# Seven block products for eight in the up projection of a decoder trunk

## The chip, the cores and the metric

The kernel runs on one core of a Trainium2 chip. The metric is the device time of one execution in microseconds; lower is better. TensorE multiplies, VectorE (DVE) and ScalarE (ACT) do the elementwise work, GpSimd (POOL) and SyncE (SP) here mostly issue DMAs.

## What is computed

One decoder layer on 512 tokens of 2048 features. The change is in its last sub-layer, a gated MLP with a short causal convolution, and in what hands over to it; the attention, the gated delta rule and the cross-attention before it keep their code.

```python
def conv_ffn(h, w_up, conv_w, conv_b, w_down):          # h (1, 512, 2048), w_up (2048, 11264)
    u = causal_dwconv(h @ w_up, conv_w) + conv_b         # 3 taps along the tokens
    gate, up = jnp.split(u, 2, axis=-1)                  # 5632 features each
    return (jax.nn.silu(gate) * up) @ w_down             # w_down (5632, 2048)
...
x = x + memory_cross_attention(rmsnorm(x, xattn_norm), mem_n, w_xq, w_xkv, w_xo)
x = x + conv_ffn(rmsnorm(x, ffn_norm), w_up, ffn_conv, ffn_conv_bias, w_down)
return rmsnorm(x, final_norm)
```

## The kernel before

Features lie on the 128 partitions, tokens along the free dimension, so that a tile is 128 features x 512 tokens. float32 accuracy is had by splitting each operand into a high part (rounded to float32r, a ScalarE copy) and a low part (the rest, a VectorE subtraction): `split` for activations, `load_w` for weights. `mm3` then makes a product of three matmuls, high x high, high x low, low x high, with the weights as the stationary operand. `load_w` loads a unit of weights (128 x 8 blocks x 128, 512 KB) into a `raw` tile (four buffers) through the SP queue and splits it into a `wh` tile (three buffers). A dense product of one feature tile over 2048 features (`dense`) is two units, 16 blocks, 48 matmuls of 512 columns.

The matmuls stand in program order (`pinned` chains them). On the other engines and on the DMA queues a scheduler sets the order when the program is built. Each engine, and each queue, works in that order: an instruction that waits holds up all behind it.

The cross-attention's output projection (`xo_part`, `xo_out`) makes 16 tiles: sum with the residual in `x4`, split of `x4 * g_ffn` into `x3hl`, and the sum of squares for the norm, whose factor `rs` is applied to the results of the up projection. The residual tiles `x4` (8 tiles of two) stay in the pool `hlB`, `x3hl` (16 tiles) in `hlA`.

The MLP then runs in six groups of gate features, 8, 8, 8, 8, 8 and 4 tiles of the 44. For each tile `ffn_mm` multiplies gate and up, `ffn_act` applies the norm and the convolution, and silu(gate) * up is split into `ghl`, in SBUF. After each group `down` adds its part of the down projection to all 16 tiles of `x4`: for each tile one unit of weights, 24 matmuls. The last group works in two halves of the tokens (`h0`, `h1`, 256 columns), with the first three blocks of some tiles ahead of the last gate, and ends in the final norm and the stores.

Of the kernel before, what the change touches and what calls it, by code (L numbers as in the profile page):

```python
# [34 lines left out]
def trunk(ctx, tc, xT, memT, w_in, w_first, w_ba, w_out, w_xq, w_xkv, w_xo, w_up, w_down,  # L35
# [868 lines left out]
    def ffn_act(f, ps, tag):
        y = fp.tile([P, S + 2], F32, tag="y", name="y", bufs=2)
# [1 line left out]
        dve.tensor_tensor(y[:, 2:], ps, rs, ALU.mult)
# [1 line left out]
        c = fp.tile([P, S], F32, tag=tag, name="c", bufs=2)
# [39 lines left out]
    groups = [(0, 8), (8, 16), (16, 24), (24, 32), (32, 40), (40, 44)]
    gate_next = None  # L950
    for gi, (f0, f1) in enumerate(groups):
        last = gi == len(groups) - 1
        for f in range(f0, f1):
            pg_ = ffn_mm(f) if gate_next is None else gate_next
            gate_next = None
            if f == 0:
                pu_ = ffn_mm(FT + f)
                drain()
                pb.close()
                fp = open_pool(ctx, "fp")  # L960
                ssq = fp.tile([P, S], F32, name="ssq4")
            g = ffn_act(f, pg_, "gate")
            act.activation(g, g, AF.Silu)
            if f:
                pu_ = ffn_mm(FT + f)
            u = ffn_act(FT + f, pu_, "up")
            dve.tensor_tensor(g, g, u, ALU.mult)
            if f % 10 < 8:
                t = hlB.tile([P, 2, S], F32R, tag="hl", name="ghl")
            else:  # L970
                t = fp.tile([P, 2, S], F32R, tag="ghl", name="ghl", bufs=2)
            split(t[:, 0], t[:, 1], g)
            ghl[f] = hl(t)
# [116 lines left out]
```

## Time and profile before

| | |
|---|---|
| median of 3 runs | 2573.16 us (2572.33 to 2577.62) |
| the profiled execution: its own time, its span | 2573.16 us, 2571.3 us |
| granted TensorE clock, mean | 0.997 |
| TensorE busy | 2541.5 us, 99% |
| VectorE, ScalarE, GpSimd busy | 54%, 38%, 6% |
| DMA | 293.05 MB, mean 114 GB/s |

Busy shares are of the span, which is the stretch from the first to the last instruction. Matmuls overlap in a pipeline, so the duration of one (some 0.39 us) is longer than the distance between two; the distance is read from the chain of work that ended last. In the rows PE is TensorE, L90 is the line of all dense matmuls, L141 and L143 split weights, L128, L129, L131 and L132 split activations, L910 and L912 are the convolution.

### The profile page before, as it was taken

The page shows a single profiled execution, that of the slowest core. Times are in us where ns is not written, and L with a number is a line of the kernel's source. Part 1 is how long each engine was busy: PE and PEld are TensorE (multiplying, and loading weights), DVE is VectorE, ACT ScalarE, POOL GpSimd, SP SyncE. Part 2 cuts the span into 40 slices and gives each one's busy share as a digit, 9 for nine tenths or more (in the row PEclk, how much of TensorE's full clock was granted, in tenths as well). Part 3 has the DMA queues.
Part 4 walks back from the last instruction along what each step waited for, and adds up shares of the span by engine and source line. Part 5 has one row for each costly group of instructions (what it writes and reads, how often), then busy time and mean ns, then how long its engine had stood idle before and what let it go on. Part 6 is the DMA issues. An engine that isn't in the chain of part 4 may idle for free.

```text
span 2571.3 us, 31857 instructions
## 1 busy us (share of the span) xinstructions
PE 2541.5 (99%) x12108; PEld 2109.7 (82%) x12108; DVE 1380.4 (54%) x2529; ACT 968.4 (38%) x1637; POOL 158.3 (6%) x426
## 2 busy tenths in 40 slices
PE   9999999999999999999999999999999999999997
PEld 7888877888887888888888888888888888888887
DVE  6766566666665446764444544444435543444356
ACT  5645434545554335543322332233223321332135
POOL 1111022212201000000000000000000000000000
PEclk9999999999999999999999999999999999999999
DMA  5444443333335445332232223222222222222332
GB/s 204 131 140 130 135 143 106 117 108 111 108 111 193 147 151 189 105 109 99 99 98 95 94 99 99 94 95 98 99 96 94 98 99 96 94 98 99 97 102 81
DMA packets 93243, 293.05 MB, mean 114 GB/s; under 512 B 12209, under 2 KB 17649, under 8 KB 93089
## 3 DMA queue, kind: packets, MB, share of 16 engines
q1 hardware_dynamic: 68960, 238.06, 28.2%
q0 software_dynamic: 12544, 33.00, 4.4%
q10 hardware_dynamic: 11584, 19.96, 2.1%
q8 instruction: 95, 1.56, 0.2%
q14 instruction: 60, 0.48, 0.1%
HBM read 266.29 MB, written 24.67 MB: 113 GB/s over the span
## 4 chain that ended last, share of the span: by engine, by line
PE 68%; DVE 1%; DMA 0%; ACT 0%; issue 0%; DVEq 0%; POOLq 0%; SPq 0%; ACTq 0%
PE psg L90 28%; PE psd L90 23%; PE pss L90 17%; DMA raw<-in_w_down 0%; DVE x L926 0%; PE pss L93 0%; DMA m<-mixed 0%; DVE wl L143 0%; DVE c L912 0%; DVE mhl L129 0%; ACT wl L141 0%; ACT e L813 0%; DMA xo<-in_xT 0%; DVE ghl L129 0%; ACT mhl L128 0%
## 5 line engine op out<-in xcount | busy, mean ns | idle before, releaser
L141 ACT ACTIVATE wh<-raw 128x1024 fp32r<-128x1024 f32 x424 | 449.7, 1061 | 1039.0 <-PE psg L90 362.8
L143 DVE TENSOR_TENSOR wh<-raw,wh 128x512 fp32r<-128x512 f32 x848 | 552.1, 688 | 337.7 <-ACT wh L141 337.2
L90 PE MATMUL psd<-xhl,wh 128*128 128x512 f32 x1824 | 470.0, 402 | 0.0
L90 PE MATMUL psg<-x3hl,wh 128*128 128x512 f32 x1824 | 416.5, 389 | 0.0
L90 PEld LDWEIGHTS psg<-x3hl,wh 128*128 128x128 f32 x1824 | 342.5, 188 | 71.4 <-issue 0.5
L90 PEld LDWEIGHTS psd<-xhl,wh 128*128 128x128 f32 x1824 | 331.0, 189 | 62.3 <-issue 0.5
L90 PE MATMUL psd<-x3hl,wh 128*128 128x512 f32 x1200 | 274.1, 389 | 0.0
L90 PE MATMUL pss<-x3hl,wh 128*128 128x512 f32 x1200 | 274.1, 389 | 0.0
L90 PEld LDWEIGHTS psd<-x3hl,wh 128*128 128x128 f32 x1200 | 225.3, 188 | 46.7
L90 PEld LDWEIGHTS pss<-x3hl,wh 128*128 128x128 f32 x1200 | 225.3, 188 | 46.7
L90 PE MATMUL pss<-xhl,wh 128*128 128x512 f32 x864 | 204.5, 392 | 0.0
L90 PE MATMUL psg<-ghl,wh 128*128 128x512 f32 x816 | 189.3, 392 | 0.0
L90 PEld LDWEIGHTS pss<-xhl,wh 128*128 128x128 f32 x864 | 160.7, 188 | 33.7
L90 PEld LDWEIGHTS psg<-ghl,wh 128*128 128x128 f32 x816 | 153.2, 188 | 34.0
L912 DVE SCALAR_TENSOR_TENSOR c<-y,fcv,c 128x512 f32<-128x512 f32 x176 | 131.8, 749 | 4.0 <-ACT c L910 1.0
L90 PE MATMUL pss<-ghl,wh 128*128 128x512 f32 x552 | 128.6, 392 | 0.0
L90 PE MATMUL psd<-ghl,wh 128*128 128x512 f32 x552 | 128.4, 391 | 0.0
L90 PE MATMUL psd<-mhl,wh 128*128 128x512 f32 x528 | 121.8, 390 | 1.6 <-DVE mhl L129 1.1
L90 PEld LDWEIGHTS pss<-ghl,wh 128*128 128x128 f32 x552 | 103.6, 188 | 23.0
L90 PEld LDWEIGHTS psd<-ghl,wh 128*128 128x128 f32 x552 | 103.6, 188 | 22.9
L90 PEld LDWEIGHTS psd<-mhl,wh 128*128 128x128 f32 x528 | 98.9, 188 | 23.4 <-DVE mhl L129 1.8
L906 POOL MEMSET y<- 128x2 f32 x88 | 8.7, 99 | 1484.5 <-DVE c L912 1358.0
(297 smaller groups left out, 2362.1 us busy)
## 6 DMA issues: line engine op xcount, KB each, us to landing
raw<-in_w_up SPq DMA_DIRECT2D x176, 512.0 KB, 3.3
raw<-in_w_in SPq DMA_DIRECT2D x104, 512.0 KB, 3.5
raw<-in_w_down SPq DMA_DIRECT2D x88, 512.0 KB, 3.3
raw<-in_w_out SPq DMA_DIRECT2D x32, 512.0 KB, 3.3
raw<-in_w_xkv SPq DMA_DIRECT2D x16, 512.0 KB, 3.9
kqv<-c ACTq DMA_DIRECT2D x24, 256.0 KB, 3.6
kqv_t<-kqv POOLq DMA_DIRECT2D x16, 256.0 KB, 3.1
xo<-in_xT POOLq DMA_DIRECT2D x16, 256.0 KB, 3.6
```

Of the source, the lines that this page charges most:

```text
L90: pinned(nc.tensor.matmul(out, a, b, start=start, stop=stop), c)
L141: act.activation(parts[0], raw, AF.Copy)
L143: dve.tensor_tensor(parts[1][:, c], raw[:, c], parts[0][:, c].bitcast(F32), ALU.subtract)
L906: pool.memset(y[:, 0:2], 0.0)
L912: dve.scalar_tensor_tensor(c, y[:, j:j + S], w[:, j:j + 1], c, ALU.mult, ALU.add)
```

## The change

Take the matrix product of a gate tile and an up tile with x as one of 2 x 2 blocks: rows of the result are gate and up, the inner dimension is cut into its first and second 1024 features, the tokens into their first and second 256. A11, A12 are the two units of the gate's weights, A21, A22 those of the up tile's. Strassen's scheme in Winograd's form needs seven block products (p1 to p7) where the plain product has eight, and 15 sums: four of W, four of x, seven of products.

- `quad(f)` does this for the pairs 3 to 43. Of the sums of W three are made by DMAs that add into SBUF (`accum_op`, issued from GpSimd's queue): A21 + A22 in `sa1`, A21 - A11 in `sa3` (on top of a ScalarE copy of -A11), and `a22 += sa3`. The fourth, `a12 -= a22`, is a VectorE operation. Each of the seven blocks of weights is split into high and low as before. Each product is 24 matmuls of 256 columns.
- `x_sums(j)` makes the sums of x (`T12`, `T34`) from the normed x, which `xo_out` now also stores to DRAM (`x3sd`), while the first three pairs are multiplied in the plain way. For this `xo_out` has one more VectorE operation, into `xs`, which also includes the earlier norm's factor `rs2`; `ffn_rs` divides it out again with a reciprocal.
- The gates go to DRAM (`gd`), and so does the residual (`x3d`), since `T12` and `T34` take the 16 tiles of `hlB`. The down projection starts when all pairs are done: `load_g` reads the gates back and splits them, group by group.
- In the last group all weights are kept in `hlA` and `hlB`.

```diff
+    x3d = [dram.tile([P, 2, S], F32, name=f"x3d{i}") for i in range(KT // 2)]
+    x3sd = [dram.tile([P, S], F32, name=f"x3s{i}") for i in range(KT)]
+    gd = [dram.tile([P, S], F32, name=f"g{i}") for i in range(FT)]
...
     def xo_out(f, ps):
         dve.tensor_tensor(x4[f], x4[f], ps, ALU.add)
+        xs = bp.tile([P, S], F32, tag="xold", name="xs", bufs=3)
+        dve.scalar_tensor_tensor(xs, x4[f], g_ffn[:, f:f + 1], rs2, ALU.mult, ALU.mult)
+        dma3(out=x3sd[f], in_=xs)
         t = hlA.tile([P, 2, S], F32R, tag="hl", name="x3hl")
-        split(t[:, 0], t[:, 1], x4[f], g_ffn[:, f:f + 1])
+        split(t[:, 0], t[:, 1], xs)
         add_sq(ssq, x4[f], f == 0, bp)
+        if f % 2:
+            dma3(out=x3d[f // 2], in_=x4p[f // 2])
...
+    def ffn_rs():
+        for _ in rstd(rs, ssq, bp):
+            pass
+        dve.reciprocal(rs2, rs2)
+        dve.tensor_tensor(rs, rs, rs2, ALU.mult)
...
+    def x_sums(j):
+        b = fp.tile([P, 2, S], F32, tag="raw2", name="xb", bufs=4)
+        for i in range(2):
+            dma2(out=b[:, i], in_=x3sd[j + 8 * i])
+        q = fp.tile([P, 4, 256], F32, tag="raw2", name="xq4", bufs=4)
+        bq = b.rearrange("p a (c s) -> p (a c) s", c=2)
+        dve.tensor_tensor(q[:, 0::2], bq[:, 1:2].broadcast_to([P, 2, 256]), bq[:, 0::3], ALU.subtract)
+        dve.tensor_tensor(q[:, 1], bq[:, 3], q[:, 0], ALU.subtract)
+        dve.tensor_tensor(q[:, 3], bq[:, 2], q[:, 1], ALU.subtract)
+        for i, T in enumerate((T12, T34)):
+            t = hlB.tile([P, 2, 2, 256], F32R, tag="hl", name="xt")
+            split(t[:, :, 0], t[:, :, 1], q[:, 2 * i:2 * i + 2])
+            T += [t]
...
+    def prod(raw, xs):
+        wh = w_parts(raw)
+        ps = dbank()[:, :256]
+        for j in range(8):
+            mm3(ps, blk_(wh, j), xs(j), j == 0, j == 7)
+            tick()
+        return ps
...
+    def quad(f):
+        u2, u3 = (fq.tile([P, 256], F32, tag=t, name=t, bufs=1) for t in ("u2", "u3"))
+        a11 = raw_w(w_up[f, 0], wp, "raw")
+        sa1 = raw_w(w_up[FT + f, 0], wp, "raw")
+        dma2(out=sa1, in_=w_up[FT + f, 1], accum_op=ALU.add)
+        a22 = raw_w(w_up[FT + f, 1], fp, "raw2")
+        a12 = raw_w(w_up[f, 1], fp, "raw2")
+        sa3 = fq.tile([P, 8, P], F32, tag="sa3", name="sa3", bufs=1)
+        act.activation(sa3, a11, AF.Copy, scale=-1.0)
+        dma2(out=sa3, in_=w_up[FT + f, 0], accum_op=ALU.add)
+        yg, yu = ffn_y("g"), ffn_y("u")
+        p1 = prod(a11, part_x(0, h0))
+        act.activation(u2, p1, AF.Copy)
+        p5 = prod(sa1, part_t(T12, 0))
+        p4 = prod(a22, part_t(T34, 1))
+        dma2(out=a22, in_=sa3, accum_op=ALU.add)
+        p2 = prod(a12, part_x(8, h0))
+        dve.tensor_tensor(yg[:, 2:258], p2, u2, ALU.add)
+        dve.tensor_tensor(a12, a12, a22, ALU.subtract)
+        p7 = prod(sa3, part_t(T34, 0))
+        p6 = prod(a22, part_t(T12, 1))
+        dve.tensor_tensor(u2, p6, u2, ALU.add)
+        dve.tensor_tensor(u3, p7, u2, ALU.add)
+        dve.tensor_tensor(yu[:, 2:258], p4, u3, ALU.add)
+        dve.tensor_tensor(yu[:, 258:], p5, u3, ALU.add)
+        dve.tensor_tensor(yg[:, 258:], p5, u2, ALU.add)
+        dve.tensor_tensor(yu[:, 2:], yu[:, 2:], rs, ALU.mult)
+        cu = ffn_conv(FT + f, yu, "up")
+        p3 = prod(a12, part_x(8, h1))
+        dve.tensor_tensor(yg[:, 258:], yg[:, 258:], p3, ALU.add)
+        dve.tensor_tensor(yg[:, 2:], yg[:, 2:], rs, ALU.mult)
+        ffn_g(f, ffn_conv(f, yg, "gate"), cu)
...
+    def load_g(f, i):
+        if f % 2 == 0:
+            r = fp.tile([P, 2, S], F32, tag="raw2", name="graw", bufs=4)
+            for j in range(2):
+                dma(out=r[:, j], in_=gd[f + j])
+                t = (hlA if i % 2 else hlB).tile([P, 2, S], F32R, tag="hl", name="ghl")
+                split(t[:, 0], t[:, 1], r[:, j])
+                ghl[f + j] = hl(t)
```

**Place 1: VectorE in the middle of the up projection.** Before, part of a pair's work looks like this, `wh` being weights, `y` the normed product, `c` the convolution:

```order
L143 TENSOR_TENSOR wh_18626<-raw_18624,wh_18626 128x512 x2
L912 SCALAR_TENSOR_TENSOR c_18546<-y_18543,fcv_559,c_18546 128x512 x2
L967 TENSOR_TENSOR c_18477<-c_18477,c_18546 128x512
L129 TENSOR_TENSOR ghl_18551<-c_18477,ghl_18551 128x512
L143 TENSOR_TENSOR wh_18656<-raw_18654,wh_18656 128x512 x2
L907 TENSOR_TENSOR y_18615<-pss_18554,rs3_9816 128x512
L143 TENSOR_TENSOR wh_18698<-raw_18696,wh_18698 128x512 x2
```

Now, around the start of a quad, `raw_11577` is its `sa1`, `raw_11580` its `a22`, `raw_11582` its `a12`; `y_11352` and `y_11350` are up and gate of the quad before:

```order
L132 TENSOR_TENSOR wh_11620<-raw_11577,wh_11620 128x1024
L936 SCALAR_TENSOR_TENSOR c_11532<-y_11352,fcv_627,c_11532 128x512
L1016 TENSOR_TENSOR y_11350<-y_11350,psd_11539 128x256
L936 SCALAR_TENSOR_TENSOR c_11532<-y_11352,fcv_627,c_11532 128x512
L1017 TENSOR_TENSOR y_11350<-y_11350,rs3_9884 128x512
L132 TENSOR_TENSOR wh_11648<-raw_11580,wh_11648 128x1024
L132 TENSOR_TENSOR wh_11677<-raw_11582,wh_11677 128x1024
L936 SCALAR_TENSOR_TENSOR c_11566<-y_11350,fcv_627,c_11566 128x512 x2
L132 TENSOR_TENSOR wh_11707<-sa3_11584,wh_11707 128x1024
L941 TENSOR_TENSOR c_11566<-c_11566,c_11532 128x512
L1005 TENSOR_TENSOR raw_11582<-raw_11582,raw_11580 128x1024
L132 TENSOR_TENSOR wh_11735<-raw_11580,wh_11735 128x1024
```

The rest of the quad before now stands between the splits for p5, p4, p2 and p7, and `a12 -= a22` (L1005) stands directly ahead of the split for p6.

**Place 2: the POOL queue in the middle of the up projection.** Before, it had only the two zero columns ahead of each tile of `y`:

```order
L906 MEMSET y_14046 128x2
L906 MEMSET y_14118 128x2
L906 MEMSET y_14187 128x2
L906 MEMSET y_14259 128x2
L906 MEMSET y_14328 128x2
```

Now, for the same quad (`sa3_11584`, its `a22` in `raw_11580`), with `raw_12051` the `sa1` of two quads later:

```order
L928 MEMSET y_11350 128x2
L996 DMA sa3_11584<-in_w_up 128x1024
L928 MEMSET y_11589 128x2
L991 DMA raw_12051<-in_w_up 128x1024
L1002 DMA raw_11580<-sa3_11584 128x1024
L928 MEMSET y_11587 128x2
L996 DMA sa3_11821<-in_w_up 128x1024
```

Three adding DMAs a quad are new on this queue, and `a22 += sa3` (L1002) stands right behind the add into the `sa1` of two quads later (L991).

**Place 3: VectorE at the end of the cross-attention's output projection.** Before, the last tiles of `x3hl` are made like this:

```order
L871 TENSOR_TENSOR x4_9040<-x4_9040,psd_10178 128x512
L143 TENSOR_TENSOR wh_10231<-raw_10229,wh_10231 128x512 x2
L132 SCALAR_TENSOR_TENSOR x3hl_10192<-x4_9040,nrm_161,x3hl_10192 128x512
L189 TENSOR_TENSOR ssq3_9815<-ssq3_9815,sq_10195 128x512
L143 TENSOR_TENSOR wh_10272<-raw_10270,wh_10272 128x512 x2
```

Now:

```order
L874 TENSOR_TENSOR x4_9108<-x4_9108,psd_10298 128x512
L132 TENSOR_TENSOR x3hl_10292<-xs_10289,x3hl_10292 128x512
L192 TENSOR_TENSOR ssq3_9883<-ssq3_9883,sq_10295 128x512
L877 SCALAR_TENSOR_TENSOR xs_10312<-x4_9108,nrm_229,rs2_8701 128x512
L192 TENSOR_TENSOR ssq3_9883<-ssq3_9883,sq_10318 128x512
L146 TENSOR_TENSOR wh_10355<-raw_10353,wh_10355 128x512 x2
L911 RECIPROCAL rs2_8701<-rs2_8701 128x512
L132 TENSOR_TENSOR x3hl_10315<-xs_10312,x3hl_10315 128x512
```

Each tile has its step into `xs` (L877) more, and the reciprocal stands ahead of the low half of the last tile.

## Rows read from the trace of the kernel before

**Rows 1.** The page's head and its first part: busy us, share, instructions.

```profile
span 2571.3 us, 31857 instructions
PE 2541.5 (99%) x12108; PEld 2109.7 (82%) x12108; DVE 1380.4 (54%) x2529; ACT 968.4 (38%) x1637; POOL 158.3 (6%) x426
```

**Rows 2.** Stretches: output projection of the cross-attention, up, down, last group.

```profile
core 0: us, PE busy (x) PEld busy (x) DVE busy (x) ACT busy (x) POOL busy (x), PEclk, DMA share, GB/s
1074.70:1112.90 38.20, 38.20 (x167) 31.10 (x167) 37.51 (x61) 27.31 (x40) 0.00 (x0) 1.00 0.25 83
1656.00:1824.00 168.00, 168.00 (x743) 139.09 (x742) 84.89 (x126) 54.32 (x63) 1.59 (x16) 1.00 0.30 96
2360.00:2440.00 80.00, 80.00 (x350) 65.35 (x349) 28.74 (x44) 15.93 (x15) 0.00 (x0) 1.00 0.29 94
2520.00:2556.00 36.00, 36.00 (x301) 35.95 (x301) 25.89 (x64) 25.68 (x58) 0.00 (x0) 1.00 0.17 59
```

**Rows 3.** Chain that ended last: start us, us, what; 256, 512 and 256 columns.

```profile
1024.55 4.07 PE psd L90 x34
...
1165.17 32.64 PE psg L90 x144
...
2524.30 2.88 PE psd L90 x24
```

**Rows 4.** Groups by form, up projection, 1660 to 1825: busy us, mean ns, idle before.

```profile
L141 ACT ACTIVATE wh<-raw 128x1024 fp32r<-128x1024 f32 x31 | 32.9, 1062 | 74.9 <-PE psg L90 29.7 <-PE psd L90 25.4 <-PE pss L90 19.8
...
L910 ACT ACTIVATE c<-y,fbs,fcv 128x512 f32<-128x512 f32 x15 | 12.0, 801 | 0.0
...
L963 ACT ACTIVATE c<-c 128x512 f32<-128x512 f32 x8 | 5.1, 632 | 16.8 <-DVE c L912 16.8
```

**Rows 5.** Timeline of VectorE, end of the output projection: start us, us, instruction.

```profile
1107.78 0.75 DVE L132 SCALAR_TENSOR_TENSOR x3hl<-x,nrm,x3hl 128x512 fp32r<-128x512 f32 x1
1108.44 0.69 DVE L189 TENSOR_TENSOR ssq<-ssq,sq 128x512 f32<-128x512 f32 x1
...
1112.11 0.75 DVE L132 SCALAR_TENSOR_TENSOR x3hl<-x,nrm,x3hl 128x512 fp32r<-128x512 f32 x1
1112.77 0.69 DVE L189 TENSOR_TENSOR ssq<-ssq,sq 128x512 f32<-128x512 f32 x1
```

**Rows 6.** Timeline of VectorE: merged rows of several instructions of one kind.

```profile
1126.31 1.54 DVE L912 SCALAR_TENSOR_TENSOR c<-y,fcv,c 128x512 f32<-128x512 f32 x2 [1.02 <-ACT c L910]
...
2502.60 4.30 DVE L143 TENSOR_TENSOR wl<-raw,wl 128x512 fp32r<-128x512 f32 x7
...
2517.14 0.78 DVE L931 TENSOR_TENSOR x<-x,pss 128x256 f32<-128x256 f32 x2
```

**Rows 7.** One line's or group's durations: reciprocal, scan, a 256-wide copy.

```profile
L815 DVE RECIPROCAL sm<-sm x8: 157/166/166, 1015.2 to 1043.5; 128x2 f32<-128x2 f32 x8
...
L668 DVE TENSOR_TENSOR_SCAN r<-ones,a 128x512 f32<-128x512 f32 x8 | 9.7, 1208 | 0.0
...
L188 ACT ACTIVATE sq<-x 128x256 f32<-128x256 f32 x26 | 10.7, 415 | 9.1 <-DVE x L931 9.1
```

**Rows 8.** DMA queues (packets, MB, share) and issues (KB each, us to landing).

```profile
q1 hardware_dynamic: 68960, 238.06, 28.2%
q0 software_dynamic: 12544, 33.00, 4.4%
...
raw<-in_w_up SPq DMA_DIRECT2D x176, 512.0 KB, 3.3
...
x<-x2d POOLq DMA_DIRECT2D x8, 512.0 KB, 8.7
...
tnd<-tnat POOLq DMA_DIRECT2D x1, 512.0 KB, 3.4
```

**Rows 9.** Timeline of POOL, its DMA issues one by one.

```profile
994.07 0.53 POOL L794 DMA_DIRECT2D x<-x2d  x1 [0.15 <-issue]
994.75 0.53 POOL L794 DMA_DIRECT2D x<-x2d  x1 [0.15 <-issue]
```

**Rows 10.** A stretch with full DMA queues, columns as in rows 2.

```profile
1000.00:1005.00 5.00, 5.00 (x35) 4.61 (x34) 2.18 (x4) 1.58 (x2) 0.00 (x0) 1.00 1.03 417
```

**Rows 11.** Timeline of TensorE, start of the first up block.

```profile
1109.73 8.78 PE L90 MATMUL psg<-x3hl,wh 128*128 128x512 f32 x38
1118.35 1.02 PE L90 MATMUL pss<-ssq,cst 128*128 128x512 f32 x2
```

**Rows 12.** Waits of TensorE, 2503 to 2518: us in total, times, longest.

```profile
PE psg L90 <- ACT ghl L128: 0.5, 1, 0.5
PE psg L90 <- DVE ghl L129: 0.3, 1, 0.3
```

More of the change, by code (lines that the diff above doesn't have):

```diff
@@ L751, in trunk @@
         x2hl.append(hl(t))
-    rs = bp.tile([P, S], F32, name="rs2")
+    rs = rs2 = bp.tile([P, S], F32, name="rs2")
     spawn(rstd(rs, ssq, bp), 8.0)
@@ L892, in trunk @@
     drain()
-    banks[0] = "ddgggss"
-    spawn(rstd(rs, ssq, bp), 8.0)
-    fp = None
+    banks[0] = "ddgggsss"
+    def ffn_rs():
[3 more added lines that the diff above has]
+        dve.tensor_tensor(rs, rs, rs2, ALU.mult)
+        return
+        yield
+    spawn(ffn_rs(), 8.0)
+    fp, fq = None, None
+    pf = ctx.enter_context(ExitStack())
+    h0, h1 = slice(0, 256), slice(256, S)
     def ffn_mm(f):
@@ L902, in ffn_mm, with ffn_y, ffn_conv @@
         return ps
[L904 to L905 removed]
+    def ffn_y(tag):
+        y = fq.tile([P, S + 2], F32, tag="y" + tag, name="y", bufs=1)
         pool.memset(y[:, 0:2], 0.0)
[L907 removed]
+        return y
+    def ffn_conv(f, y, tag):
         w = fcv[:, f]
[L909 removed]
+        c = fq.tile([P, S], F32, tag=tag, name="c", bufs=1)
         act.activation(c, y[:, 2:], AF.Identity, scale=w[:, 2:3], bias=fbs[:, f:f + 1])
@@ L913, in ffn_act, with ffn_g @@
         return c
+    def ffn_g(f, c, u):
+        act.activation(c, c, AF.Silu)
+        dve.tensor_tensor(c, c, u, ALU.mult)
+        dma3(out=gd[f], in_=c)
+    T12, T34 = [], []
+    def x_sums(j):
[11 more added lines that the diff above has]
+            T += [t]
@@ new lines, in w_parts, with part_x, part_t @@
+    def w_parts(raw):
+        t = wp.tile([P, 2, 8, P], F32R, tag="wh", name="wh", bufs=3)
+        split(t[:, 0], t[:, 1], raw)
+        return (t[:, 0], t[:, 1])
+    def prod(raw, xs):
[5 more added lines that the diff above has]
+        return ps
+    def part_x(k0, c):
+        return lambda j: (x3hl[k0 + j][0][:, c], x3hl[k0 + j][1][:, c])
+    def part_t(T, i):
+        return lambda j: (T[j][:, i, 0], T[j][:, i, 1])
@@ new lines, in raw_w @@
+    def raw_w(src, pl, tag):
+        r = pl.tile([P, 8, P], F32, tag=tag, name="raw", bufs=4)
+        dma(out=r, in_=src)
+        return r
+    def quad(f):
[30 more added lines that the diff above has]
+        ffn_g(f, ffn_conv(f, yg, "gate"), cu)
@@ new lines, in trunk @@
+    NS = 3
+    for f in range(NS):
+        pg_ = ffn_mm(f)
+        if f == 0:
+            pu_ = ffn_mm(FT + f)
+            drain()
+            pb.close()
+            fp = open_pool(ctx, "fp")
+            fq = open_pool(pf, "fq")
+        yg = ffn_y("g")
+        dve.tensor_tensor(yg[:, 2:], pg_, rs, ALU.mult)
+        cg = ffn_conv(f, yg, "gate")
+        for j in ((0, 1), (3, 4), (6, 7))[f]:
+            x_sums(j)
+        if f:
+            pu_ = ffn_mm(FT + f)
+        yu = ffn_y("u")
+        dve.tensor_tensor(yu[:, 2:], pu_, rs, ALU.mult)
+        ffn_g(f, cg, ffn_conv(FT + f, yu, "up"))
+        for j in ((2,), (5,), ())[f]:
+            x_sums(j)
@@ new lines, in trunk @@
+    for f in range(NS, FT):
+        quad(f)
+    banks[0] = "ddgggss"
+    pf.close()
+    fq = open_pool(ctx, "fr")
+    ssq = fq.tile([P, S], F32, name="ssq4")
+    x4, x4p = [], []
+    ghl = [None] * FT
+    def load_g(f, i):
[6 more added lines that the diff above has]
+                ghl[f + j] = hl(t)
@@ L917, in finish_rms @@
             tc.keep_in_program_order(act.preload_act_table_set("natural_log_exp_and_others"))
-        for _ in rstd(rs[:, c], ssq[:, c], fp):
+        for _ in rstd(rs[:, c], ssq[:, c], fq):
             pass
@@ L946, in down @@
             down_out(f, ps, c, last)
-    ghl = [None] * FT
     groups = [(0, 8), (8, 16), (16, 24), (24, 32), (32, 40), (40, 44)]
-    gate_next = None
     for gi, (f0, f1) in enumerate(groups):
-        last = gi == len(groups) - 1
         for f in range(f0, f1):
[L954 to L973, printed above, removed]
+            load_g(f, gi)
+        if gi == 0:
+            for i in range(KT // 2):
+                t = hlB.tile([P, 2, S], F32, tag="hl", name="x4")
+                dma(out=t, in_=x3d[i])
+                x4 += [t[:, 0], t[:, 1]]
+                x4p.append(t)
         n = f1 - f0
         per = 8 // n
-        if not last:
-            gate_next = ffn_mm(f1)
+        if gi < len(groups) - 1:
             for fb in range(KT):
@@ L981, in trunk @@
     whs, ahead = [], []
-    h0, h1 = slice(0, 256), slice(256, S)
     for fb in range(KT // per):
-        wh = [hlA.tile([P, 8, P], F32R, tag="hl", name="wl") for _ in range(2)]
+        wh = [(hlA if fb < 6 else hlB).tile([P, 8, P], F32R, tag="hl", name="wl") for _ in range(2)]
         load_w(w_down[gi][fb], 8, wh)
```

2 lines of the change are left out of this document (1 added, 1 removed).

## The prediction

> **What bounds the kernel now.** I read the page's first part, then stretches of the span, then the chain that ended last. TensorE is busy for 99% of the span [rows 1], and at 38.20 of 38.20, 168 of 168, 80 of 80 and 36 of 36 us in stretches of the cross-attention's output projection, the up projection, the down projection and the last group, at a granted clock of 1.00, which is the level of 2.4 GHz, all the time [rows 2]. VectorE has half of its time free in the up projection (84.89 of 168 us), ScalarE two thirds, the DMA engines 0.30 busy [rows 2]. So only TensorE's time counts, as long as every other engine delivers. Its price is in the chain: 144 matmuls of 512 columns take 32.64 us, 0.2267 us each; of 256 columns, 24 take 2.88 and 34 take 4.07 us, 0.120 each, a little more than half [rows 3].
>
> **Term 1, seven products for eight.** A pair of feature tiles (gate and up) is now 96 matmuls of 512 columns: 96 x 0.2267 = 21.76 us. A `quad` is 7 products x 8 blocks x 3 matmuls = 168 of 256 columns: 168 x 0.120 = 20.16 us. So of the eighth that the algorithm promises (2.72 us) 1.60 us are left, since each matmul has a part that doesn't shrink with its columns. The first three pairs stay as they are, 41 become quads: **41 x 1.60 = -65.6 us**. This goes to the end only if TensorE is still never waiting, so the rest is about who feeds it within 20.16 us.
>
> The rule here comes from the Trainium skill, "TensorE: Matmul & The Clock Gate", section "Back-to-back issue gap": warm matmuls of 512 and 256 columns come 518 and 262 cycles apart, 216 and 109 ns. By it a quad would save 96 x 216 - 168 x 109 = 2.4 us and 41 of them 99 us. The rows say 227 and 120, and I go by them.
>
> **Supply by engine.** Prices on VectorE are spacings, not durations: seven splits of 512 columns in 4.30 us, the last lasting 0.69, make 0.60 each; two 256-wide sums in 0.78 us make 0.36 [rows 6]; 0.24 us more for each 256 columns gives an estimate of 1.1 us for 1024. A scalar-tensor-tensor is followed after 0.66 us (1107.78 to 1108.44) [rows 5]. A quad on VectorE: seven low halves of weights and the subtraction from `a12`, 8 x 1.1; seven 256-wide sums of products, 7 x 0.36; three 512-wide operations, 3 x 0.60; four conv steps, 4 x 0.66; in sum 15.8 us, 78% of 20.16 (before 51%). ScalarE: seven high halves and the copy into `sa3`, 8 x 1.06, two conv starts of 0.80, Silu 0.63, one 256-wide copy of 0.4 us [rows 7]: 11.1 us, 55% [rows 4]. DMA: a 512 KB load is 28.2% of the span times 0.524/238.06 MB = 1.6 us of all 16 engines [rows 8]; four of them, 0.8 for the gate's store, and three adds at 2.9 (below) make 15.9 of 20.16 us. Nothing is full, so what decides is lateness.
>
> **Lateness within a quad.** Let 0 be TensorE's start of the first product; the order is p1 at 0, p5 2.88, p4 5.76, p2 8.64, p7 11.52, p6 14.40, p3 17.28. There are three buffers of split weights, so a split can begin when the product three places ahead has ended. VectorE's rows around the quad's start (place 1 of the order above) run: the sums that need p6 begin at -2.7, five 256-wide ones, yu x rs, the split for p5 (ends about 1.2, with 0.1 us more for each of four pairs in which the second reads the first: two conv steps take 1.54 us, not 1.41 [rows 6]), two conv steps, two operations on yg, the split for p4: it ends at 4.6, needed at 5.76. The splits for p2 and p7 have 2 to 3 us to spare, in the same manner. Only p6 is different: its weights are `a22` after the adding DMA `a22 += sa3`, which may not start before p4's split has read `a22` (4.6). It stands on the POOL queue behind `sa1` of two quads later (place 2), which waits for its own load: buffer free at 1.2, landing 3.3 us later [rows 8], 4.5. POOL takes 0.68 us from one issue to the next (994.07 to 994.75) [rows 9], so both adds are in flight from 4.5 and 5.2 on, one behind the other. Behind the landing VectorE must do `a12 -= a22` and p6's low half, 2.2 us, so it has to land by 14.4 - 2.2 = 12.2. While VectorE waits there, p3's split and the sums of p6 queue behind it, all needed later than p6.
>
> **Term 2, the adding DMAs.** No row has one. A plain 512 KB POOL transfer takes 3.4 us alone [rows 8], and when the queues are full 417 GB/s make 1.26 us of 512 KB [rows 10], so some 2.1 us are fixed. With S for the streaming of one add, the second lands at 4.5 + 2.1 + 2 S; the limit 12.2 is met up to S = 2.8 us. Lower end: S = 1.26, as a plain copy, no stall. Upper end: an add has to read two sources, so twice the software queue's mean, 4.4% of the span x 0.524/33.00 MB = 1.8 us [rows 8], S = 3.6: lands 13.8, 1.6 us of stall a quad, 66 us in all. I take two reads at the mean of the full queue's rate and the load queue's (1.26 and 1.6), S = 2.86: it lands at 12.3, 0.12 us late, **41 x 0.12 = +5 us**. The row that is nearest for a burst of POOL transfers, x4 read back, lands after 8.7 us at the median [rows 8], and that is eight in a row beside weights.
>
> "Collectives: The Full Stack", section "The bandwidth ceiling: the fold count and why AG ≠ RS ≠ AR", in the Trainium skill says that an add in the DMA engine costs nothing itself but has two source reads on one ring, so half the rate; by it S is 2.5 us and this term 0. No run here shows an add yet.
>
> **Term 3, the output projection of the cross-attention.** VectorE is already the limit there: 37.51 of 38.20 us [rows 2]. The change gives it one more operation for each of 16 tiles (place 3): 16 x 0.60 = 9.7 us, and a RECIPROCAL ahead of the last low half, whose only row has 2 columns; I bound it by 0.6 and by the slowest 512-wide VectorE row, 1.2 us [rows 7]. The last `x3hl` ended at 1112.77 + 0.09 = 1112.86 [rows 5]; it becomes 1123.8. TensorE's first up block starts at 1109.9, needs that tile for its last three matmuls, 45 x 0.2267 and the norm's 0.86 us later, at 1121.0 [rows 11]. **+2.8 us** (2.2 at the least).
>
> By the Trainium skill, "VectorE: DVE Perf Modes", section "First, the fixed hardware budget", the reciprocal is an iterative divide with a repeat count of 8, which would make it an estimated 4.3 us and this term 6.
>
> **Term 4, the seams.** The wait of the last group for the last gate, 0.5 + 0.3 us, goes [rows 12]: **-0.8**; almost all of it was hidden before by work done ahead. A new seam is between the last quad and down. On VectorE eight low halves of gates stand between the last quad's sums and the first down weights; from p6's end: 17.4, gates until 18.8, five sums and yu x rs to 21.1, one sum of p3 and half a weight split to 22.1, against TensorE's 20.16: **+2.0** (0 to 3.5). In the three unchanged pairs the sums of x add 8 x 2.5 = 20 us of VectorE to 3 x 9.6, in 65 us: hidden, 0. In the down phase the gates are read back and split, 8 in 87 us, which were split in the up phase: hidden, 0.
>
> **Sum.** -65.6 + 5 + 2.8 - 0.8 + 2.0 = -56.6. The profiled execution has a span of 2571.3 us [rows 1] and took 2573.16, 1.9 more, which is also the median of the three runs: 2573.2 - 56.6 = 2516.6, so **2517 us**. A measurement of this kernel can tell about 0.2%, 5 us.
>
> **Rivals.**
> - *Adds so slow that the change loses.* Place: `a22 += sa3` before p6. Without stall in quads the change is worth 61.6 us, 1.5 us a quad; a landing of 13.7, S = 3.55, eats that. If reading both sources and writing don't overlap, S = 3 x 1.26 = 3.8: lands 14.2, 2.0 us a quad, 82 us: 2594 us. For it: the software queue's own mean is the slowest of the rates, two adds sit right behind each other, and the budget is spent by my middle value already. Against it: nothing else is loaded between 4.5 and 10.9, when p6's split frees the next buffer. Chance 0.18.
> - *A partial stall* of 0.6 to 1.3 us a quad (S from 3.1 to 3.45): 2536 to 2566 us. Chance 0.15.
> - *VectorE becomes the bound.* At 78% it takes 1.28 times the prices, say if POOL's descriptor work or the extra DMA traffic slows its SBUF reads; at 1.35, 21.3 us a quad, +1.2: 2561 us and a little more by late splits. For: 0.69 us durations against 0.60 spacings leave unclear what it pays when it waits after every step. Against: the output projection ran at 98% on these spacings. Chance 0.07.
> - *A faster pace of 256-column matmuls.* 512 columns at 2.4 GHz are 213 ns and 256 are 107, so both rows have some 13 ns on top; if long streams hid all but 2 of them at 256 columns, 168 x 0.109 = 18.3 us a quad, 76 us less, 2441. Against it are two stretches at 120 ns with different operands [rows 3]. Chance 0.03. (By the skill's two figures above the gain is 33 us more than mine.)
> - The forecast, stall of at most 0.6 us a quad: 0.57, with a range of its own from 2509 (terms 2, 3 and 4 at their low ends) to 2536.
>
> Range: leaving out the fast rival and the most of the losing one, 2507 to 2580: S = 3.6 gives 2578, and 0.05 us in a quad's price is 2 us on either side. Faster by over 0.2%: 0.57 + 0.15 + 0.03 = 0.75. Within 0.2%: 0.05, and slower 0.20, from the losing rival and the tail of the VectorE one.
>
> **What would show it.** TensorE: 24 matmuls in 2.88 us in the quads' products, and the chain there made of TensorE alone. A period of 20.2 to 20.3 us from quad to quad; if it is longer, TensorE's wait stands before p6 and is ended by the split of `a22`, and behind that by the DMA. VectorE 78 to 88% busy in the stage. Adds landing within 7 us of issue. A wait of 2 to 3 us in the first up block, 2 us at the first down unit, none at the last group. The prediction is wrong if an add takes over 8 us from issue to landing, if the wait is before another product than p6 (then my walk through VectorE's order is wrong), or if 256-column matmuls are not 0.120 us apart.

## The result, and the profile after

The changed kernel takes 2657.88 us (median of 4 runs, 2651.9 to 2660.42) against 2573.28 (2572.33 to 2577.62): ratio 1.0316, 95% interval 1.0302 to 1.0329, 84 us slower. The forecast was 2517 us. The profiled execution has a span of 2654.5 us. First its head and first part; [rows 1] show the same of the kernel before.

```profile
span 2654.5 us, 39125 instructions
PE 2541.6 (96%) x15060; PEld 2251.1 (85%) x15060; DVE 1675.3 (63%) x2874; ACT 1147.1 (43%) x1858; POOL 273.4 (10%) x565
```

TensorE is busy for as long as before (2541.6 against 2541.5 us), although each quad should be 1.6 us cheaper, and 113 us of its span are idle where before there were 30. The stretches, with the columns of [rows 2]: before the quads, the quads, the down phase.

```profile
1130.00:1190.00 60.00, 57.03 (x245) 46.73 (x244) 48.43 (x83) 29.04 (x38) 11.94 (x26) 0.97 0.73 228
1600.00:2000.00 400.00, 368.78 (x2858) 361.98 (x2857) 281.83 (x375) 177.70 (x205) 47.13 (x85) 0.94 0.68 168
2300.00:2500.00 200.00, 200.00 (x884) 165.67 (x883) 80.15 (x123) 46.36 (x49) 0.00 (x0) 1.00 0.33 101
```

The loss is in the quads. A quad has 168 matmuls, so 2858 of them in 400 us mean a period of 168 x 400 / 2858 = 23.5 us for 20.16. The middle row splits it: 31.2 us of waits, and 368.8 us for 2858 matmuls that at 0.120 us would take 343.0, so 25.8 us lost to the granted clock, 0.94 for 1.00. In 17.0 quads that is 1.84 us of waits and 1.52 us of clock each; 3.36 x 41 = 138 us. No other engine is full (VectorE is busy for 281.8 of 400 us), nor are the DMA engines (0.68).

TensorE's waits (us in total, times, longest):

```profile
PE pss L93 <- ACT wh L131: 18.1, 11, 2.5
PE psg L93 <- DVE wh L146: 13.4, 5, 4.7
PE psg L93 <- ACT wh L131: 13.3, 12, 2.4
PE psd L93 <- ACT wh L131: 11.1, 6, 3.0
PE psg L93 <- DVE wh L132: 10.6, 14, 0.8
...
```

L131 (high half) and L132 (low half) are the split of weights in the quads; the waits for L146 lie outside of the quads. Where in the quad it is late shows the timeline of TensorE: start us, us, instruction, idle before it.

```profile
1296.87 3.04 PE L93 MATMUL psg<-xt,wh 128*128 128x256 f32 x24
1302.40 0.68 PE L93 MATMUL pss<-xt,wh 128*128 128x256 f32 x2 [2.49 <-ACT wh L131]
1303.67 5.06 PE L93 MATMUL pss<-xt,wh 128*128 128x256 f32 x22 [0.59 <-DVE wh L132]
```

After p7 TensorE waits 2.49 us for the high half and 0.59 for the low half of p6's weights, the place that the prediction named. What it did not name is the third row: p6's 22 remaining matmuls take 5.06 us, which at 0.120 are 2.64. The chain that ended last, from one p6 (1257.12) to the next:

```profile
1257.12 4.24 PE pss L93 x22
...
1261.38 0.44 DVE u L1008
...
1263.98 1.15 DVE wh L132
1265.14 3.62 DMA raw<-in_w_up
...
1269.29 0.54 POOL raw L991
1269.83 7.43 DMA raw<-sa
...
1277.28 1.23 DVE raw L1005
1278.51 1.19 DVE wh L132
```

And POOL's timeline at that place, with what ended its idle time:

```profile
1269.29 0.86 POOL L991 DMA_DIRECT2D raw<-in_w_up  x1 [2.27 <-DMA raw<-in_w_up]
1269.83 1.20 POOL L1002 DMA_DIRECT2D raw<-sa  x1
```

It is a loop: p6; the sums that need it, on VectorE (L1008 to L1013); the split for `sa1` in VectorE's line behind them; the load into the buffer that this split frees; the POOL queue, which waits for that load to issue the add into it (L991) and only then can issue `a22 += sa3` (raw<-sa, L1002); `a12 -= a22` and the split for p6, which begins at 1279.74. One round is 22.6 us. The next is 23.9 (to 1303.67): p6 ran at full speed there, and VectorE reached the sums only after two splits, which ended just after p6; the load took 5.5 us in place of 3.6, and the add 8.2. Before, the chain in this stage was TensorE alone [rows 3]. The issues of DMAs (KB each, median us to landing):

```profile
raw<-in_w_up SPq DMA_DIRECT2D x176, 512.0 KB, 4.8
...
raw<-in_w_up POOLq DMA_DIRECT2D x41, 512.0 KB, 5.6
raw<-sa POOLq DMA_DIRECT2D x41, 512.0 KB, 8.1
```

A load of W lands after 4.8 us at the median (3.3 before [rows 8]), the add for p6 8.1 us after its issue. Over 8 us was one of the signs of being wrong that the prediction names.

### The profile page after: what moved, and what is told of

The parts are those of the page before. It is cut to its first block, busy times and chain, and to the rows that moved or that the text cites. A ratio compares the mean times of both kernels' runs of the same rounds, so it can differ in the third digit from the quotient of the medians.

```text
span 2654.5 us, 39125 instructions
## 1 busy us (share of the span) xinstructions
PE 2541.6 (96%) x15060; PEld 2251.1 (85%) x15060; DVE 1675.3 (63%) x2874; ACT 1147.1 (43%) x1858; POOL 273.4 (10%) x565
## 3 DMA queue, kind: packets, MB, share of 16 engines
q0 software_dynamic: 31536, 101.69, 18.2%
## 4 chain that ended last, share of the span: by engine, by line
PE 49%; DMA 20%; DVE 13%; issue 3%; ACT 1%; POOL 1%; POOLq 0%; DVEq 0%; ACTq 0%; SPq 0%
PE psd L93 23%; PE psg L93 16%; DMA raw<-sa 12%; PE pss L93 9%; DMA raw<-in_w_up 7%; DVE wh L132 4%; DVE raw L1005 2%; DVE y L1013 1%; POOL raw L991 1%; DVE u L1009 1%; DMA xb<-x3s 1%; DVE y L1010 1%; DVE wh L146 1%; DVE u L1008 1%; PE pss L96 1%
## 5 line engine op out<-in xcount | busy, mean ns | idle before, releaser
L144 ACT ACTIVATE wh<-raw 128x1024 fp32r<-128x1024 f32 x260 | 275.3, 1059 | 555.9 <-PE psd L93 192.8
L146 DVE TENSOR_TENSOR wh<-raw,wh 128x512 fp32r<-128x512 f32 x520 | 340.7, 688 | 147.7 <-ACT wh L144 144.1
L131 ACT ACTIVATE wh<-raw 128x1024 fp32r<-128x1024 f32 (+1 forms) x262 | 263.9, 1024 | 362.9 <-DMA raw<-sa 235.6
L132 DVE TENSOR_TENSOR wh<-raw,wh 128x1024 fp32r<-128x1024 f32 (+1 forms) x262 | 307.6, 1189 | 24.9 <-ACT wh L131 24.5
L93 PE MATMUL pss<-xt,wh 128*128 128x256 f32 x1488 | 209.2, 301 | 28.0 <-ACT wh L131 18.1
L93 PEld LDWEIGHTS pss<-xt,wh 128*128 128x128 f32 x1488 | 199.8, 208 | 33.7 <-ACT wh L131 20.6
L93 PE MATMUL psg<-xt,wh 128*128 128x256 f32 x1440 | 199.8, 298 | 24.0 <-ACT wh L131 13.3
L93 PEld LDWEIGHTS psg<-xt,wh 128*128 128x128 f32 x1440 | 190.5, 205 | 29.6 <-ACT wh L131 16.0
L1005 DVE TENSOR_TENSOR raw<-raw 128x1024 f32<-128x1024 f32 x41 | 50.3, 1226 | 216.5 <-DMA raw<-sa 216.5
L93 PE MATMUL psg<-x3hl,wh 128*128 128x256 f32 (+1 forms) x1224 | 166.2, 294 | 3.0 <-DVE wh L146 3.0
L93 PEld LDWEIGHTS psg<-x3hl,wh 128*128 128x128 f32 x1224 | 158.7, 194 | 7.6 <-DVE wh L146 3.4
```

The source lines that it names most:

```text
L93: pinned(nc.tensor.matmul(out, a, b, start=start, stop=stop), c)
L144: act.activation(parts[0], raw, AF.Copy)
L146: dve.tensor_tensor(parts[1][:, c], raw[:, c], parts[0][:, c].bitcast(F32), ALU.subtract)
L1005: dve.tensor_tensor(a12, a12, a22, ALU.subtract)
```

## The experiments

All kernels are the changed one with the edit shown. Ratios are to runs of the kernel before on the same chip: 2573.8 us for e1 to e4, 2574.1 for e5 to e8, 2576.1 for e9 and e10, 2574.0 for e12.

**e1_swap: `a22 += sa3` goes ahead of the add into `sa1` of two quads later, on the POOL queue.** Nothing else in the source differs; the scheduler now also sets ScalarE's copy into `sa3` (L995 in the changed kernel) ahead of the high half of p6's weights, as in e5 and e12, which makes p6's path 1 us longer, not shorter.

```
+        adds[f] = dma2(out=a22, in_=sa3, accum_op=ALU.add)
...
+        i1 = dma2(out=sa1, in_=w_up[FT + f, 1], accum_op=ALU.add)
+        if f - 2 in adds:
+            tc.add_manual_dep(i1.ins, adds[f - 2].ins.name,
+                              mybir.DependencyInfo(mybir.DependencyClass.NoSync, mybir.DependencyReason.DATA),
+                              reason="queue order")
```

> Only the place of one adding DMA on the POOL queue changes: `a22 += sa3` goes ahead of the add into the `sa1` of two quads later. Theory (the add that p6 waits for stands behind a load and another add): its landing comes about 5.6 us after p4's split instead of some 13, TensorE's wait in the quads goes, with it the dips of the clock, the quads' period falls from 23.7 to 20.2 to 20.6 us, and the time to 2515 to 2545 us. Rival 1 (adds are slow because the DMA engines are too full, whatever their order): the landing stays above 8 us, the time above 2620. Rival 2 (VectorE is too full for 20 us): no change, 2650 to 2660.

2524.54 us, ratio 0.980 (0.9781 to 0.9819): 133 us less than the change by the order of two DMAs. Its issues and its stretch in the quads:

```profile
raw<-in_w_up POOLq DMA_DIRECT2D x41, 512.0 KB, 7.2
raw<-sa POOLq DMA_DIRECT2D x41, 512.0 KB, 4.9
...
1200.00:2020.00 820.00, 820.00 (x6836) 820.00 (x6835) 676.47 (x894) 434.99 (x493) 109.81 (x199) 1.00 0.78 195
```

TensorE is never idle in 820 us, at a clock of 1.00. The same three adds are made; the DMA engines are even busier (0.78), since the quads run faster. The `sa1` add now lands late instead (7.2), and TensorE doesn't wait for it.

**e2_dve: `a22 += sa3` by VectorE.**

```
-        dma2(out=a22, in_=sa3, accum_op=ALU.add)
+        dve.tensor_tensor(a22, a22, sa3, ALU.add)
```

> `a22 += sa3` becomes a VectorE operation of 1.1 us; the other two adds stay DMAs. Theory of the late add: the period falls to 20.2 to 20.6 us, time 2515 to 2540 us. Rival 1 (full DMA engines): a part of the gain, since a third of the adds is gone, 2580 to 2620. Rival 2 (VectorE is the bound): 41 x 1.1 = 45 us slower than the change, about 2700.

2525.08 us, 0.9809 (0.979 to 0.9828). VectorE does more and TensorE still doesn't wait:

```profile
1600.00:2000.00 400.00, 400.00 (x3335) 400.00 (x3335) 347.46 (x456) 212.15 (x239) 37.10 (x79) 1.00 0.65 168
```

At 347 of 400 us, 87%, VectorE is not the bound, so that rival falls.

**e3_noadds: the three adding DMAs left out** (the sums of W are incomplete).

```
-        dma2(out=sa1, in_=w_up[FT + f, 1], accum_op=ALU.add)
-        dma2(out=sa3, in_=w_up[FT + f, 0], accum_op=ALU.add)
-        dma2(out=a22, in_=sa3, accum_op=ALU.add)
```

> All three adding DMAs are left out (the sums of W are then incomplete, so the output is not the layer's); VectorE, ScalarE and TensorE do all that they did. Theory of the late add: no wait in the quads at all, granted clock 1.00 there, period 20.2 us, time 2510 to 2530 us; this is the floor for this order of work. Rival 2 (VectorE): the period stays above 22 us and the time above 2600.

2519.01 us, 0.9783 (0.9767 to 0.9799). Next to e1_swap, three adds a quad in a good order cost 5.5 us in all by the medians; the runs of the two overlap (2517.6 to 2527.2 and 2515.7 to 2522.8), so it may be less.

**e4_plain: no quads**; all pairs are computed as the first three, and the rest of the change stays.

```
-    NS = 3
+    NS = FT
```

> No quads: all 44 pairs are multiplied in the plain way, everything else of the change stays (normed x and its sums, gates through DRAM, down as its own phase). It prices the rest of the change by itself. By the waits of the changed kernel outside the quads, 3.4 us in the output projection, 3.0 before the third pair and about 7 at the seam to down, and a little for the clock after each: 2580 to 2592 us. If the rest of the change costs a good part of the 84 us, it is above 2600.

2579.61 us, 1.0025 (1.0015 to 1.0035): what lies around the quads costs 5.8 us. (The wait at the seam behind the quads, 2 us in e1_swap, isn't among it: TensorE doesn't wait there in this run.) The quads without adds (e3_noadds) gain 60.6 us on this, 1.48 for each of 41.

**e5_small, e6_oneload: which part of the queue's delay.** In e5 the add into `sa1` covers one of eight blocks; in e6 `sa1` is a plain POOL load of its second term, for which nothing else has to land.

```
-        dma2(out=sa1, in_=w_up[FT + f, 1], accum_op=ALU.add)
+        dma2(out=sa1[:, 0], in_=w_up[FT + f, 1][:, 0], accum_op=ALU.add)
...
-        sa1 = raw_w(w_up[FT + f, 0], wp, "raw")
-        dma2(out=sa1, in_=w_up[FT + f, 1], accum_op=ALU.add)
+        sa1 = wp.tile([P, 8, P], F32, tag="raw", name="raw", bufs=4)
+        dma2(out=sa1, in_=w_up[FT + f, 1])
```

> The order of the changed kernel, but the adding DMA into sa1 covers one of its eight blocks, 64 KB for 512 KB (the sum is left incomplete). The POOL queue still waits for sa1's load before it issues a22 += sa3; what is gone is the streaming of the add ahead. In the changed kernel a22 += sa3 lands 8.1 us after its issue behind a full add, with the order exchanged 4.9 us. Theory (the stall is the sum of the wait for the load and of the streaming of the add ahead, and either one without the other would nearly fit): landing about 5 us, 3 us earlier than in the changed kernel, more than the 1.9 us that TensorE waits for in a quad; period about 20.2 to 20.5 us, 2520 to 2535 us. Rival (the wait for the load alone makes the stall; the streaming matters little): landing still 7 us or more, period near 23.7 us, 2640 to 2660 us.

> The order of the changed kernel, but sa1 is a plain load of its second term on the POOL queue (the load of the first term and the addition are left out). The POOL queue has the same 512 KB ahead of a22 += sa3, but nothing on it waits for another load to land; it waits only for sa1's buffer. Theory (either part without the other nearly fits): a22 += sa3 is issued some 4 us earlier than in the changed kernel, lands about 7 to 8 us after its issue, and is in time; period 20.2 to 20.5 us, 2520 to 2535 us. Rival (the streaming of the transfer ahead alone makes the stall): period near 23.7 us, 2640 to 2660 us.

e5: 2535.18 us, 0.9843 (0.9828 to 0.9859); e6: 2522.67, 0.9802 (0.9787 to 0.9817). The POOL timeline of e5, two of one quad's three issues, and its stretch in the quads:

```profile
1260.59 0.85 POOL L991 DMA_DIRECT2D raw<-in_w_up  x1 [3.67 <-DMA raw<-in_w_up]
1261.13 1.20 POOL L1002 DMA_DIRECT2D raw<-sa  x1
...
1600.00:2000.00 400.00, 397.77 (x3304) 396.60 (x3303) 327.41 (x433) 209.04 (x238) 54.70 (x99) 1.00 0.64 171
```

It still waits for the load of `sa1`, yet `raw<-sa` lands after 4.9 us (8.1 in the change) and the period is 168 x 400 / 3304 = 20.3 us. So the wait for the load alone doesn't make the stall; the add that streams ahead is needed too. TensorE still waits now and then (397.77 busy of 400), with no loss of clock. e6 is clean but says less than its expectation: without the wait the plain load is issued 3.4 us ahead of `raw<-sa`, not 0.5, so that it streams out of the way as well (landing 4.5 us). And a plain load is a cheaper transfer than an add. So e6 doesn't separate the wait from the streaming; e12_sa1first below, with the add kept and the wait gone, comes nearer to that.

**e10_p5first: `sa1`'s product first.** A test of the loop.

```
+        p5 = prod(sa1, part_t(T12, 0))
         p1 = prod(a11, part_x(0, h0))
         act.activation(u2, p1, AF.Copy)
-        p5 = prod(sa1, part_t(T12, 0))
```

> The order of the changed kernel on all queues; in each quad the product of sa1 (p5) is computed before that of a11 (p1), so that sa1's buffer comes free one product (2.88 us) earlier in the quad. Theory (the lateness runs in a loop that feeds itself: p6, the evictions behind it on VectorE, the split of sa1, the load into the buffer that this frees, the POOL queue's wait for that load, a22 += sa3, the difference and the split, p6 again; this loop's length, 23.7 us, is the period): the split of sa1 stands one place further ahead in VectorE's line, by a split of 1.15 us at least and a product of 2.88 us at most, so the loop shortens to between 20.8 and 22.5 us, less what the higher clock gives back, up to 1.6 us: a period of 20.2 to 22 us, 2525 to 2590 us. Rival (the adds take too long from the quad's own start, wherever sa1's buffer comes free): no change, period near 23.7 us, 2640 to 2665 us.

2635.5 us, 1.0237 (1.022 to 1.0254): a miss, nearer to what the rival expected (2640), with a period of 168 x 400 / 2905 = 23.1 us. The chain still has a split of VectorE's behind p6's sums, then a load, then POOL:

```profile
1289.22 1.15 DVE wh L132
1290.38 3.69 DMA raw<-in_w_up
...
1294.61 0.54 POOL raw L991
1295.15 7.36 DMA raw<-sa
...
1600.00:2000.00 400.00, 371.57 (x2905) 365.11 (x2904) 287.87 (x385) 180.90 (x209) 48.06 (x86) 0.95 0.68 170
```

The second split of a quad is now `a11`'s. The SP queue has the load of `a11` ahead of that of `sa1`, so I took it that `sa1`'s load stood behind one that waits for `a11`'s buffer. That was tested next.

**e12_sa1first: as e10, and `sa1` is also loaded ahead of `a11`.**

```
+        sa1 = raw_w(w_up[FT + f, 0], wp, "raw")
+        dma2(out=sa1, in_=w_up[FT + f, 1], accum_op=ALU.add)
         a11 = raw_w(w_up[f, 0], wp, "raw")
-        sa1 = raw_w(w_up[FT + f, 0], wp, "raw")
-        dma2(out=sa1, in_=w_up[FT + f, 1], accum_op=ALU.add)
```

> As the kernel with p5 ahead of p1, and the load of sa1 also stands ahead of that of a11 on the SP queue. a22 += sa3 still stands behind the add into sa1 on the POOL queue. With p5 ahead of p1 alone the period stayed near 23 us: the chain of that run still ran from p6 over the evictions and a split of VectorE to the load of sa1, but the split after the evictions was now that of a11, for whose buffer the load ahead of sa1's on the SP queue waits. Theory (the loop from p6 over the evictions, the split and the SP queue to the load of sa1 is what sets the period): sa1's load now waits for a split that stands ahead of p6's evictions on VectorE, so the loop is open, a22 += sa3 is issued 4 us or more earlier, and the quads run at 20.2 to 20.5 us, 2519 to 2535 us. Rival (the adds in line take too long from the quad's own start, whichever buffer comes free first): a period of 23 us or more, 2630 to 2660 us.

2552.93 us, 0.9909 (0.9891 to 0.9927), between the two expectations, far nearer to the theory's. POOL issues the two adds at 1259.45 and 1261.62 with no load waited for, and the loop is out of the chain:

```profile
1259.45 0.85 POOL L990 DMA_DIRECT2D raw<-in_w_up  x1 [9.29 <-DVE y L1016]
...
1261.62 0.85 POOL L1002 DMA_DIRECT2D raw<-sa  x1 [1.20 <-DVE wh L132]
...
1600.00:2000.00 400.00, 389.66 (x3212) 386.13 (x3211) 315.52 (x421) 198.53 (x231) 52.64 (x97) 1.00 0.76 189
```

The period is 20.9 us. What remains against e1_swap, 28 us, is 0.7 us a quad, again before p6. `a22 += sa3` still lands late, 7.2 us after an issue that is 2.2 us behind the other add, and behind it ScalarE has the copy into `sa3` for the next quad (L995) ahead of the high half of p6's weights. VectorE's and ScalarE's timelines, and the issues:

```profile
1627.69 1.23 DVE L1005 TENSOR_TENSOR raw<-raw 128x1024 f32<-128x1024 f32 x1 [3.54 <-DMA raw<-sa]
...
1627.74 1.06 ACT L995 ACTIVATE sa<-raw 128x1024 f32<-128x1024 f32 x1 [4.92 <-issue]
1628.71 2.94 ACT L131 ACTIVATE wh<-raw 128x1024 fp32r<-128x1024 f32 x3
...
raw<-sa POOLq DMA_DIRECT2D x41, 512.0 KB, 7.2
```

The trace names no releaser for the copy here, but it begins 0.05 us after the subtraction that waits for `a22 += sa3`, and so in 37 of the 38 quads from 1200 to 2000 us; in e1_swap and e5_small the trace names that DMA as the copy's releaser. `sa3` has one buffer, and the DMA reads it, so the copy can't begin sooner. In the changed kernel p6's high half stands ahead of the copy (1277.36 and 1278.33 us); behind it, it comes 1 us later.

**e7_x4pool, e8_x4pool_xbsp, e9_xbsp: the seams of the better order.** All three have e1's order. e7 moves the eight loads of x4 before the down phase from SP to POOL; e8 does that and moves the loads of `x_sums` from POOL to SP; e9 does the latter alone.

```
-                dma(out=t, in_=x3d[i])
+                dma2(out=t, in_=x3d[i])
...
-            dma2(out=b[:, i], in_=x3sd[j + 8 * i])
+            dma(out=b[:, i], in_=x3sd[j + 8 * i])
```

> The exchanged order of the two adds (2524.5 us), and the eight loads of x from DRAM at the seam from the quads to the down projection go to the POOL queue, which is idle there, in place of the SP queue, where a load of W stands behind them. The wait of 2.0 us for W's halves in that seam should go: about 2522.5 us if that wait is all they cost (2521 to 2524); unchanged at 2524.5 if the DMA engines, not the queue, are what W waits for.

> As the one before, and the loads of the slices of x for the sums go to the SP queue in place of the POOL queue. With the exchanged order alone TensorE waits 3.2 us before the third pair of up blocks, where VectorE waits for such a load, issued on the POOL queue behind an adding DMA and landing 7.4 us later. If the queue is the cause, 3.2 us less than the one before, about 2519.5 us (2518 to 2522); if the loads then stand ahead of loads of W on SP and delay these, the same or slower (2522 to 2530).

> The exchanged order of the two adds (2524.5 us), the loads of x at the seam left on the SP queue as in the change, and only the loads of the slices of x for the sums moved from the POOL to the SP queue. In the run that moved both sets the 3.2 us wait before the third pair was gone (TensorE busy 60.00 of 60 us from 1130 to 1190), while the seam to the down projection waited some 5 us more. Expected if the two effects are separate: 3.2 us less than the exchanged order, 2521 us (2519 to 2524). If the seam's wait only moved there with the time, no gain: 2524 to 2527 us.

e7: 2531.63 us (0.981 to 0.9844), a miss: where e1 waited 2.0 us at the seam, TensorE is now idle for 7.2 (busy 52.81 of 60 us), so moving these loads off SP's line brought W no sooner. e8: 2524.3 (0.9791 to 0.9821), above the 2518 to 2522 that were expected if the POOL queue is the cause; the wait before the third pair is gone, and TensorE is idle for 7.0 us at the seam. e9: 2519.43, ratio 0.9781 (0.9766 to 0.9795), the fastest version that makes all its sums, although its interval overlaps that of e1. Its stretch before the quads has lost the wait:

```profile
1130.00:1190.00 60.00, 60.00 (x264) 49.37 (x263) 55.20 (x90) 31.38 (x42) 2.38 (x9) 1.00 0.73 240
```

## Why the prediction was wrong, step by step

**Term 1** was right in mechanism and nearly in size: in e1_swap 6836 matmuls take 820 us, 0.120 each, a period of 20.16 us, and the quads gain 1.48 us each for 1.60 (1.56 if one leaves out 3.4 us of waits at the seams, which e3_noadds has and e4_plain has not). By the gaps of isolated matmuls in "TensorE: Matmul & The Clock Gate" of the Trainium skill, section "Back-to-back issue gap", it would have been an estimated 2.4; the trace doesn't agree.

**Supply** was right. In e1_swap VectorE is busy for 676 of 820 us, 82% for the 78% worked out, the DMA engines 0.78 for 0.79.

**Term 2 is the step that failed** (+5 us forecast, some 138 measured), at its place and not by its price. The price of one add was right: the POOL queues' engine time went from 4.4% of 2571.3 us [rows 8] to 18.2% of 2654.5, 370 us for 68.7 MB (4 MB of it plain loads), 2.8 us for 512 KB against S = 2.86 (3.0 in e1_swap, where the share is 20.0% of 2520.6 us); with nothing right ahead of it, it lands after 4.9 us, which is 2.1 + 2.8. (The halved rate of the Trainium skill, "Collectives: The Full Stack", section "The bandwidth ceiling: the fold count and why AG ≠ RS ≠ AR", made that an estimated 2.5, near the row; the 0 that followed from it for this term fell with my 5.) Three things were wrong around it:
- *Loads among adds.* I let the load of `sa1` land after 3.3 us, as before; loads of W now take 4.8 at the median (3.6 and 5.5 in the two rounds of the chain). And 0.54 us behind another add, `a22 += sa3` takes 8.1 us where I had 7.1. Together 2.5 us, on a step that by my own numbers had -0.1 us to spare.
- *The loop.* I set the free buffer at 1.2 us of every quad, as if the split that frees it kept its time when p6 is late. It stands in VectorE's line behind p6's sums, so a late p6 frees the next buffer late. My own terms for the loop add up to 3.9 + 3.3 + 0.7 + 7.1 + 2.2 + 2.9 = 20.1 us; the sum should have been compared with the period, 20.16. Measured are 22.6 and 23.9 in two rounds. e5_small (a shorter add) and e12_sa1first (another split) shorten or open the loop and recover 123 and 105 of the 133 us; e10_p5first, which left the SP queue's order, 22.
- *The clock.* A stall of d us was to cost d. Here it costs nearly as much again (1.52 on 1.84 us), by the clock after it.

**Term 3** had a wrong place and size. I had +2.8 us for the last `x3hl`; in the changed kernel VectorE's line made W's low halves late instead, 4.66 and 3.39 us in the output projection:

```profile
1085.32 10.67 PE L93 MATMUL psg<-ohl,wh 128*128 128x512 f32 x34 [4.66 <-DVE wh L146]
1108.13 6.85 PE L93 MATMUL psg<-ohl,wh 128*128 128x512 f32 x22 [3.39 <-DVE wh L146]
```

Before had no wait there [rows 2]. With the clock behind these waits the loss is 12.7 us: the stretch from a wait in the attention that both kernels have to the first up block, before and now, with as many matmuls:

```profile
1022.00:1109.73 87.73, 87.40 (x527) 77.44 (x528) 68.36 (x132) 51.15 (x95) 0.00 (x0) 1.00 0.33 108
...
1019.93:1120.38 100.45, 92.08 (x528) 80.42 (x529) 76.61 (x145) 49.94 (x94) 0.00 (x0) 0.95 0.49 161
```

The term gave VectorE 9.7 us more (16 x 0.60 are 9.6) and let only the last tile feel it, although VectorE was the limit there already. The RECIPROCAL of 128x512, which I bounded by 1.2 us, takes 3.35:

```profile
1125.14 3.35 DVE L911 RECIPROCAL rs<-rs 128x512 f32<-128x512 f32 x1
```

The Trainium skill, "VectorE: DVE Perf Modes", section "First, the fixed hardware budget" (an iterative divide, 4.3 us by my estimate), was nearer.

**Term 4**: +2.0 at the seam to down is what e1_swap shows (1.35 + 0.60 us before W's low halves), and the wait of the last group is gone. The 0 for the three unchanged pairs was wrong by 3 us: a load for `x_sums` stood on POOL behind an add (e9_xbsp). Terms 3 and 4 together, +4.0, look near the 5.8 us of e4_plain, but that is luck: its output projection is 12 us longer too (99.8 us for 87.7 from the same wait), and some 5 us come back in the down phase, which no term had. There 350 matmuls took 80 us before [rows 2], 0.2286 each, and 884 now take 200, 0.2262, for 1920 of them; the cause of that is open.

**The rivals.** The losing one had the right place and end (p6, slower), but as its cause a slower add, S = 3.55 or more, and 2594 us at the most; the add was no slower than 3.0. VectorE as the bound and a faster 256-column pace both fall. With the order exchanged the change comes near the forecast: 2524.5, or 2519.4 with e9's edit, for 2517. The quads do what was said; that the rest fits is in part the luck of terms 3 and 4.

## What to carry to other kernels

When a step has little to spare, look for the loop that it closes: follow the late thing to what it frees, through every in-order line (an engine's, a DMA queue's), until it meets itself, add up the loop and compare it with the period. If it is longer, each period pays the full difference, as it did here (22.6 and 23.9 us for 20.16). A DMA queue that issues in order is such a line: here the add that waited 2.27 us for a load's landing held up the one behind it, so put the one with the nearest deadline first; that was worth 133 us.
